# The sample's norm in each FFN taken apart around the plain products, and the last norm's first half of columns squared and weighted during the second half's products

## The chip, the cores and the metric

One core of one Trainium2 chip runs the whole program in one launch. The metric is the device time of an execution in microseconds, as the median of several executions of the same program.

## The reference

One inference step of a small streaming encoder for two groups of requests: a prompt of 512 tokens and a sample of 8 x 16 = 128 tokens, 1024 columns each, all in float32. Two layers: the first mixes with stick-breaking attention and gated linear attention, the second with banded softmax attention over a cache. After each mixer stands an FFN, and at the end a last norm. What matters here:

```python
def _rmsnorm(x, g):
    xf = x.astype(jnp.float32)
    y = xf * lax.rsqrt(jnp.mean(xf * xf, axis=-1, keepdims=True) + EPS)
    return (y * g.astype(jnp.float32)).astype(x.dtype)

def _swiglu(h, wg, wu, wd):
    return (jax.nn.silu(h @ wg) * (h @ wu)) @ wd
...
        xp = xp + _swiglu(_rmsnorm(xp, norm_ffn_g[layer]), w_ffn_gate[layer], w_ffn_up[layer],
                          w_ffn_down[layer]).astype(xp.dtype)
        xs = xs + _swiglu(_rmsnorm(xs, norm_ffn_g[layer]), w_ffn_gate[layer], w_ffn_up[layer],
                          w_ffn_down[layer]).astype(xs.dtype)

    y_prompt = _rmsnorm(xp, norm_final_g)
    y_sample = _rmsnorm(xs, norm_final_g)
```

The hidden width of the FFN (`D_FF`) is 2816.

## The kernel before

**Tiling.** The 640 tokens are five blocks of 128 rows: blocks 0 to 3 are the prompt, block 4 is the sample. `xt[b]` is the residual stream of block b, as two halves of 512 columns. For a product, the normalised rows are transposed on TensorE and kept by columns: `fT[kp]`, four tiles of two chunks of 128 of the 1024 columns, each with all 640 tokens. Float32 products are made of three products of rounded halves: `split` (L286) makes a high part `wh` on ScalarE (L289) and a low part `wl` on VectorE (L290), in four buffers each, and every product is `wh` by high, `wh` by low, `wl` by high (L692 to L694 in the FFN's first part, L323 to L325 in its second).

**A norm.** `rstd_of` (L230) squares both halves of a block on ScalarE into a junk tile `sqj` and adds them up by row (L235), then a Newton step on VectorE with `Ln` and `Exp` on ScalarE between (L240 to L244) gives `r`. `norm_block` (L247) scales the rows by `r` into `h`, the first half on VectorE and the second on GpSimd (L252), transposes them with eight matmuls against an identity matrix into `tp` (L255), and scales each of the eight chunks by its `gm` into `fT`, turn about on ScalarE (L263) and VectorE (L261).

**The FFN.** `ffn` (L738) takes the hidden columns in groups of 6, 6, 6 and 4 chunks. In a group, `fast_pair` (L670) handles 256 columns of a weight matrix with a Strassen-like scheme: seven products of sums instead of eight. `operand` (L644) builds the sums of the activations (tiles `xs`, L657) and splits them (`block`, L660; `xb` or `xt`, L664 on ScalarE and L665 on VectorE); `weights` (L697) builds the sums of the weights, `sw`, on GpSimd (L699). A block named `b11` or `b21` holds the first 320 tokens, `b12` or `b22` the last 320, in which block 4, the sample, lies. The first two fast pairs of each FFN (the gate and the up matrix for the first 256 hidden columns, `mats[0]` and `mats[1]`) are not done in the fast way but by plain products, `part(0)` for the first 320 tokens and `part(1)` for the last 320 (L679; accumulators `pb`, copied out at L750 and L763). Between them stands `last_norm`, the norm of the sample's block, whose rows come late out of `out_sample` (L616; its adds into `x` are L626). Its transposes are queued on TensorE behind the last matmul of `mats[1]`'s `part(0)`. After the plain products follow `mats[2]`'s products (`py`, `px`, `pq`).

The FFN's second part, `proj_as` (L312), multiplies by `w_ffn_down` and adds into `xt` (L813), one half of 512 columns after the other, for each group of hidden columns. In the last group the second half closes block by block (`tail=TAIL`), and then `after` is called for each block. In layer 1 this is `after1` (L1187): norm of the block, `y` from both halves on VectorE with `gf`, the last norm's weights times -0.5 (L1193), and a transfer of 512 KB to the output on SyncE's queue (L1194).

**Order.** Each engine runs its instructions in one fixed order. A planner makes that order when the program is built: it simulates the engines with durations of its own and gives a free engine the ready instruction with the lowest priority number, which is the place in the written program unless `priority` sets another. `tc.issue_after` adds a place in the order behind a given instruction. Work tiles come from pools: `ws` (six buffers) holds `sqj`, `h`, `xs` and the gate and up outputs `sg` and `up`.

Of the kernel before, what the change touches and what calls it, by code (L numbers as in the profile page):

```python
# [8 lines left out]
F32 = mybir.dt.float32  # L9
# [3 lines left out]
AF = mybir.ActivationFunctionType  # L13
ALU = mybir.AluOpType
PSUM = bass.MemoryType.PSUM

P = 128
D = 1024
NB = 5
# [23 lines left out]
TAIL = 4  # L43
# [6 lines left out]
GROUPS = (6, 6, 6, 4)  # L50
# [5 lines left out]
def kernel(  # L56
# [8 lines left out]
    nc = tc.nc  # L65
# [40 lines left out]
    t5 = tagged("t5", N5)  # L106
# [112 lines left out]
        fill=0.0, base=DS - 1, channel_multiplier=-1,  # L219
    )  # L220

    xs_flat = x_sample.rearrange("b t d -> (b t) d")

    def x_rows(src_p, src_s, b):
# [5 lines left out]
    def rstd_of(xt, sb=None):  # L230

        ss = small.tile([P, 2], F32, tag="ss", name="ss")
        for i in range(2):
            j = (sb or ws)([P, 512], "sqj")
            nc.scalar.activation(j, xt[i], AF.Square, scale=1.0 / 32.0, accum_out=ss[:, i:i + 1])  # L235
        v = small.tile([P, 1], F32, tag="rv", name="rv")
        r = small.tile([P, 1], F32, tag="rr", name="rr")
        a = small.tile([P, 1], F32, tag="ra", name="ra")
        V = nc.vector
        V.tensor_scalar(v, ss[:, 0:1], ss[:, 1:2], EPS, op0=ALU.add, op1=ALU.add)  # L240
        nc.scalar.activation(r, v, AF.Ln)
        last_exp[:] = [nc.scalar.activation(r, r, AF.Exp, scale=-0.5)]
        V.tensor_scalar(a, r, r, v, op0=ALU.mult, op1=ALU.mult)
        V.tensor_scalar(r, a, -3.0, r, op0=ALU.add, op1=ALU.mult)  # L244
        return r

    def norm_block(xt, gi, hT, b, sb=None, bank=None, after=None):  # L247
        r = rstd_of(xt, sb)
        for i in range(2):
            tp = (bank or za)([P, 4, P], "tp")  # L250
            h = (sb or ws)([P, 512], "h")
            scaled = (nc.vector, nc.gpsimd)[i].tensor_scalar(h, xt[i], r, -0.5, op0=ALU.mult, op1=ALU.mult)  # L252
            with tc.issue_after(after.ins) if after else nullcontext():
                for j in range(4):
                    nc.tensor.transpose(tp[:, j, :], h[:, j * P:(j + 1) * P], ident)  # L255
            for j in range(4):
                c = 4 * i + j
                if len(hT) == 4:
                    d = hT[c // 2][:, c % 2, b * P:(b + 1) * P]
                    if j % 2:  # L260
                        nc.vector.tensor_scalar(d, tp[:, j, :], gm[:, gi, c:c + 1], None, op0=ALU.mult)  # L261
                    else:
                        nc.scalar.activation(d, tp[:, j, :], AF.Copy, scale=gm[:, gi, c:c + 1])  # L263
                    continue
                H = hT[c][:, 0, b * P:(b + 1) * P]
                L = hT[c][:, 1, b * P:(b + 1) * P]
                g = gm[:, gi, c:c + 1]
                nc.scalar.activation(H, tp[:, j, :], AF.Copy, scale=g)
                nc.vector.scalar_tensor_tensor(
                    L, tp[:, j, :], g, H.bitcast(F32), op0=ALU.mult, op1=ALU.subtract)  # L270
        return scaled

    def new_hT(nm):
        return [t5([P, 2, NT], f"{nm}{c}", F32R) for c in range(8)]
# [460 lines left out]
            out(1, 0, st["Q"], st["U"])  # L735
        return head, body, tail, part

    def ffn(l, xt, fT, after, last_norm):  # L738
        X, comb, block = operand(fT)
        c0, silu = 0, []  # L740
        for gi, G in enumerate(GROUPS):
# [34 lines left out]
            for i, (head, body, tail, part) in enumerate(mats):  # L776
                if gi == 0 and i == 1:
                    continue
                if gi == 0 and i == 0:


                    block("b11")
                    block("b21")
                    part(0)
                    last_norm(mats[1][3](0))
                    block("b12", gt_)
                    block("b22")
                    part(1)
                    mats[1][3](1)
                    mats[2][0]()  # L790
                    comb("t3", "b22", "b12")
                    block("t3")
                    comb("t1", "b12", "b11")
                    comb("t2", "b22", "t1")
                    block("t2")
                    block("t1")
                    comb("t4", "b21", "t2")
                    block("t4")
                    continue
# [9 lines left out]
            for half in range(2):  # L809
                last = half == 1 and gi == len(GROUPS) - 1  # L810

                def ev(b, ps):
                    nc.vector.tensor_add(xt[b][half], xt[b][half], ps)  # L813
                proj_as(l, w_ffn_down[l][c0 * P:(c0 + G) * P, :], 512 * half, 512, gT, ev,
                        tail=TAIL if last else 1, after=after if last else None)
            c0 += G


# [290 lines left out]
        last_scaled[:] = [norm_block(xt[b], 2, hT2, b)]  # L1109
    stack.close()  # L1110
    with ffn_pools():
        ffn(0, xt, hT, after0, lambda mm: norm_block(xt[4], 1, hT, 4, after=mm))
    hT = hT2


# [68 lines left out]
    nc.sync.dma_start(gf, norm_final_g.unsqueeze(0).to_broadcast([P, D]))  # L1184
    nc.vector.tensor_scalar(gf, gf, -0.5, None, op0=ALU.mult)

    def after1(b):  # L1187
        r = rstd_of(xt[b])
        dst = y_prompt[0, b * P:(b + 1) * P, :] if b < 4 else y_sample.rearrange("b t d -> (b t) d")
        y = t5([P, D], "y")  # L1190
        for i in range(2):
            s = slice(512 * i, 512 * i + 512)
            nc.vector.scalar_tensor_tensor(y[:, s], xt[b][i], r, gf[:, s], op0=ALU.mult, op1=ALU.mult)  # L1193
        nc.sync.dma_start(dst, y)  # L1194
    stack.close()
    with ffn_pools():
        ffn(1, xt, hT, after1, lambda mm: norm_block(xt[4], 3, hT, 4, after=mm))


# [37 lines left out]
```

## Time and profile before

| | |
|---|---|
| Median of three executions | 1778.29 us (1778.0 to 1786.5) |
| The profiled execution | 1781.72 us, of which its span 1780.0 us |
| Mean granted TensorE clock | 0.979 |
| TensorE busy | 1697.9 us, 95% of the span |
| VectorE, ScalarE, GpSimd busy | 1108.4, 812.0, 317.7 us |
| Chain that ended last | PE 82%, DVE 11%, ACT 3%, issue 2%, DMA 2% |
| First half of FFN 0's plain products | from 439.80 us |
| First half of FFN 1's plain products | from 1321.03 us |
| Last matmul | 1768.15 us |

All times in the profile's rows count from the first instruction. In the rows, PE is TensorE's matmuls, PEld its loads of weights, DVE VectorE, ACT ScalarE, POOL GpSimd, SP SyncE, and a q behind an engine's name its queue. A row of a timeline has the start, the duration, the engine, the line of the kernel, the operation with output and inputs, shapes, and a count of like instructions in a row; in brackets stands how long the engine was idle before it and what ended that.

### The profile page before, as it was taken

The numbers are of one execution on the slowest core, as the hardware profiler recorded it, in microseconds if no ns is written. First come the engines' busy times: TensorE is split into PE (matmuls) and PEld (weight loads), VectorE is DVE, ScalarE is ACT, GpSimd is POOL, SyncE is SP. The second block draws the span as 40 slices with busy tenths as digits, with TensorE's granted clock in tenths as the row PEclk, the third lists the DMA queues.
The fourth block names the chain that finished last, engine by engine and source line by source line (L and its number), as shares of the span: only waits on it lengthen the run. The fifth ranks groups of instructions, "written<-read, shape, count | busy, mean of one in ns | idle before, by whom it ended". The sixth has DMA issues, their size and how long they took to land.

```text
span 1780.0 us, 31737 instructions
## 1 busy us (share of the span) xinstructions
PE 1697.9 (95%) x12520; PEld 1522.9 (86%) x12520; DVE 1108.4 (62%) x2237; ACT 812.0 (46%) x1805; POOL 317.7 (18%) x339
## 2 busy tenths in 40 slices
PE   7999999998889999999999999999787999999997
PEld 7898997896788998989898889888567889899896
DVE  6466586765684765856555654755647837658465
ACT  6454435455552543534454433534536525335253
POOL 2000000000241413414110000001104224043130
PEclk9999998999899999999999999999998999999999
DMA  5311131574122222222343233368822313222212
GB/s 144 97 56 49 56 97 54 186 244 155 59 77 90 71 96 71 73 95 70 122 134 99 83 96 108 116 211 300 311 98 62 105 60 95 83 83 73 93 60 83
DMA packets 157173, 192.09 MB, mean 108 GB/s; under 512 B 12976, under 2 KB 109248, under 8 KB 157024
## 3 DMA queue, kind: packets, MB, share of 16 engines
q1 hardware_dynamic: 153440, 178.40, 30.8%
q0 software_dynamic: 3584, 11.67, 2.1%
q8 instruction: 98, 1.61, 0.4%
q14 instruction: 51, 0.42, 0.1%
HBM read 175.75 MB, written 14.29 MB: 107 GB/s over the span
## 4 chain that ended last, share of the span: by engine, by line
PE 82%; DVE 11%; ACT 3%; issue 2%; DMA 2%; SPq 0%; DVEq 0%; ACTq 0%
PE pn L323 6%; PE pn L325 6%; PE pn L324 6%; PE pw L304 5%; PE pw L305 5%; PE pw L306 5%; DVE wl L290 3%; PE px L692 3%; PE px L693 3%; PE px L694 3%; PE kttp L535 2%; PE py L694 2%; PE pm L356 2%; PE pm L359 2%; PE pm L358 2%
## 5 line engine op out<-in xcount | busy, mean ns | idle before, releaser
L290 DVE TENSOR_TENSOR wl<-raw,wh 128x512 fp32r<-128x512 f32 (+1 forms) x370 | 289.0, 788 | 251.0 <-ACT wh L289 248.5
L289 ACT CAST wh<-raw 128x512 fp32r<-128x512 f32 (+1 forms) x370 | 227.8, 618 | 377.7 <-PE pn L325 163.4
L699 POOL TENSOR_TENSOR sw<-raw 128x512 f32<-128x512 f32 x80 | 128.5, 1610 | 533.2 <-DMA raw<-in_w_ffn_gate_dram 298.2
L324 PE MATMUL pn<-wl,gT 128*128 128x512 f32 x440 | 171.2, 389 | 0.0
L289 ACT CAST wh<-sw 128x512 fp32r<-128x512 f32 x160 | 99.4, 621 | 154.9 <-PE px L693 64.4
L325 PE MATMUL pn<-wh,gT 128*128 128x512 f32 x440 | 169.3, 389 | 0.0
L323 PE MATMUL pn<-wh,gT 128*128 128x512 f32 x440 | 166.8, 389 | 0.0
L290 DVE TENSOR_TENSOR wl<-sw,wh 128x512 fp32r<-128x512 f32 x160 | 120.7, 758 | 52.6 <-ACT wh L289 41.4
L694 PE MATMUL py<-xb,wl 128*128 128x320 f32 x320 | 100.6, 314 | 9.2 <-DVE wl L290 9.2
L694 PE MATMUL pq<-xt,wl 128*128 128x320 f32 x320 | 98.8, 310 | 4.0 <-DVE wl L290 4.0
L692 PE MATMUL pq<-xt,wh 128*128 128x320 f32 x320 | 99.1, 310 | 2.2 <-ACT wh L289 2.2
L692 PE MATMUL px<-xt,wh 128*128 128x320 f32 x320 | 98.9, 309 | 0.0
L693 PE MATMUL pq<-xt,wh 128*128 128x320 f32 x320 | 98.9, 309 | 0.0
L693 PE MATMUL px<-xt,wh 128*128 128x320 f32 x320 | 98.9, 309 | 0.0
L694 PE MATMUL px<-xt,wl 128*128 128x320 f32 x320 | 98.9, 309 | 0.0
L693 PE MATMUL py<-xb,wh 128*128 128x320 f32 x320 | 98.8, 309 | 0.0
L692 PE MATMUL py<-xb,wh 128*128 128x320 f32 x320 | 98.8, 309 | 0.0
L325 PEld LDWEIGHTS pn<-wh,gT 128*128 128x128 f32 x440 | 82.6, 188 | 16.9
L324 PEld LDWEIGHTS pn<-wl,gT 128*128 128x128 f32 x440 | 82.6, 188 | 16.9
L323 PEld LDWEIGHTS pn<-wh,gT 128*128 128x128 f32 x440 | 82.3, 188 | 16.6
L304 PE MATMUL pw<-hTa,wh 128*128 128x320 f32 (+1 forms) x272 | 89.9, 331 | 0.0
L305 PE MATMUL pw<-hTa,wh 128*128 128x320 f32 (+1 forms) x272 | 88.9, 327 | 0.0
(329 smaller groups left out, 4721.5 us busy)
## 6 DMA issues: line engine op xcount, KB each, us to landing
raw<-in_w_ffn_gate_dram SPq DMA_DIRECT2D x44, 512.0 KB, 3.8
raw<-in_w_ffn_up_dram SPq DMA_DIRECT2D x44, 512.0 KB, 3.7
raw<-in_w_ffn_down_dram SPq DMA_DIRECT2D x44, 512.0 KB, 3.3
kr<-in_cache_c_k_dram SPq DMA_DIRECT2D x64, 256.0 KB, 5.4
vr<-in_cache_c_v_dram SPq DMA_DIRECT2D x16, 1024.0 KB, 7.0
raw<-in_w_in_ab_dram SPq DMA_DIRECT2D x24, 512.0 KB, 3.8
raw<-in_w_qkv_c_dram SPq DMA_DIRECT2D x24, 512.0 KB, 3.8
vr<-in_cache_a_v_dram SPq DMA_DIRECT2D x8, 1024.0 KB, 5.6
```

Of the source, the lines that this page charges most:

```text
L289: nc.scalar.copy(H, rawv)
L290: nc.vector.tensor_sub(L, rawv, H.bitcast(F32))
L304: MM(ps[i], lhsT=H[:, k % 4, :], rhs=hT[k][:, 0, s], start=(k == 0), stop=False)
L305: MM(ps[i], lhsT=H[:, k % 4, :], rhs=hT[k][:, 1, s], start=False, stop=False)
L306: MM(ps[i], lhsT=L[:, k % 4, :], rhs=hT[k][:, 0, s], start=False, stop=(k == 7))
L323: MM(ps[b], lhsT=lhs[k][:, 0, bs], rhs=H, start=(k == 0), stop=False)
L324: MM(ps[b], lhsT=lhs[k][:, 0, bs], rhs=L, start=False, stop=False)
L325: MM(ps[b], lhsT=lhs[k][:, 1, bs], rhs=H, start=False, stop=(k == K - 1))
L692: MM(ps, lhsT=H[:, k, :], rhs=X[x][0][k], start=(first and k == 0), stop=False, **f)
L693: MM(ps, lhsT=H[:, k, :], rhs=X[x][1][k], start=False, stop=False, **f)
L694: last = MM(ps, lhsT=L[:, k, :], rhs=X[x][0][k], start=False, stop=(k == 3), **f)
L699: nc.gpsimd.tensor_tensor(t, a, b, op=op)
```

## The change

**The sample's norm in each FFN.** `rstd_of` gives its second part to a function `newton`. `norm_block` is taken apart into `norm_rows` (squares, Newton step, scaling by `r`) and `norm_columns` (transposes and scaling by `gm`). In `ffn`, `last_norm` is now a pair: the rows are written ahead of `block("b11")` and of all plain products, with both halves scaled on VectorE (`ROWS`) rather than one on GpSimd; the columns are written behind `mats[0]`'s `part(0)`, with the transposes queued behind its last matmul, so that `mats[1]`'s `part(0)` stands between the transposes and the splits of `b12` and `b22`. Both FFNs have this.

**The last norm.** A new function `half1` is called for each block in layer 1 when the first half of 512 columns of the last group is added: it squares that half and multiplies it in place by `gf`. `after1` squares the second half and does the Newton step. The output is written for all five blocks behind the last block's Newton step: the first half by a scaled copy on ScalarE, the second by one instruction on VectorE, both in place, with a transfer of 256 KB for each half rather than one of 512 KB for both.

```diff
+    ROWS = (nc.vector, nc.vector)
...
+        newton(ss, r)
+        return r
+
+    def newton(ss, r):
         v = small.tile([P, 1], F32, tag="rv", name="rv")
...
-    def norm_block(xt, gi, hT, b, sb=None, bank=None, after=None):
+    def norm_rows(xt, sb=None, engines=None):
+
         r = rstd_of(xt, sb)
+        hs = []
         for i in range(2):
+            h = (sb or ws)([P, 512], "h")
+            scaled = (engines or (nc.vector, nc.gpsimd))[i].tensor_scalar(
+                h, xt[i], r, -0.5, op0=ALU.mult, op1=ALU.mult)
+            hs.append(h)
+        return hs, scaled
+
+    def norm_block(xt, gi, hT, b, sb=None, bank=None):
+        hs, scaled = norm_rows(xt, sb)
+        norm_columns(hs, gi, hT, b, bank)
+        return scaled
+
+    def norm_columns(hs, gi, hT, b, bank=None, after=None):
+
+        for i, h in enumerate(hs):
             tp = (bank or za)([P, 4, P], "tp")
-            h = (sb or ws)([P, 512], "h")
-            scaled = (nc.vector, nc.gpsimd)[i].tensor_scalar(h, xt[i], r, -0.5, op0=ALU.mult, op1=ALU.mult)
             with tc.issue_after(after.ins) if after else nullcontext():
...
                 if gi == 0 and i == 0:
+                    rows = last_norm[0]()
                     block("b11")
                     block("b21")
-                    part(0)
-                    last_norm(mats[1][3](0))
+                    last_norm[1](rows, part(0))
+                    mats[1][3](0)
                     block("b12", gt_)
                     block("b22")
                     part(1)
...
                 proj_as(l, w_ffn_down[l][c0 * P:(c0 + G) * P, :], 512 * half, 512, gT, ev,
-                        tail=TAIL if last else 1, after=after if last else None)
+                        tail=TAIL if last else 1,
+                        after=after if last else first_half if gi == len(GROUPS) - 1 else None)
...
+    def final(nm, n=1):
+        return [small.tile([P, n], F32, tag=nm, bufs=NB, name=nm) for _ in range(NB)]
+
+    ssf, rf = final("ssf", 2), final("rf")
+
+    def square(b, i):
+        j = ws([P, 512], "sqj")
+        nc.scalar.activation(j, xt[b][i], AF.Square, scale=1.0 / 32.0, accum_out=ssf[b][:, i:i + 1])
+
+    def half1(b):
+
+        square(b, 0)
+        nc.vector.tensor_mul(xt[b][0], xt[b][0], gf[:, :512])
+
     def after1(b):
-        r = rstd_of(xt[b])
-        dst = y_prompt[0, b * P:(b + 1) * P, :] if b < 4 else y_sample.rearrange("b t d -> (b t) d")
-        y = t5([P, D], "y")
-        for i in range(2):
-            s = slice(512 * i, 512 * i + 512)
-            nc.vector.scalar_tensor_tensor(y[:, s], xt[b][i], r, gf[:, s], op0=ALU.mult, op1=ALU.mult)
-        nc.sync.dma_start(dst, y)
+        square(b, 1)
+        newton(ssf[b], rf[b])
+        if b < NB - 1:
+            return
+        for b in range(NB):
+            dst = y_prompt[0, b * P:(b + 1) * P, :] if b < 4 else y_sample.rearrange("b t d -> (b t) d")
+            x = xt[b]
+            nc.scalar.activation(x[0], x[0], AF.Copy, scale=rf[b])
+            nc.sync.dma_start(dst[:, :512], x[0])
+            nc.vector.scalar_tensor_tensor(x[1], x[1], rf[b], gf[:, 512:], op0=ALU.mult, op1=ALU.mult)
+            nc.sync.dma_start(dst[:, 512:], x[1])
     stack.close()
     with ffn_pools():
-        ffn(1, xt, hT, after1, lambda mm: norm_block(xt[4], 3, hT, 4, after=mm))
+        ffn(1, xt, hT, after1, (lambda: norm_rows(xt[4], engines=ROWS)[0],
+                              lambda rows, mm: norm_columns(rows, 3, hT, 4, after=mm)), half1)
```

Layer 0's call of `ffn` changes in the same way, without `half1`.

More of the change, by code (lines that the diff above doesn't have):

```diff
@@ L235, in rstd_of @@
             nc.scalar.activation(j, xt[i], AF.Square, scale=1.0 / 32.0, accum_out=ss[:, i:i + 1])
+        r = small.tile([P, 1], F32, tag="rr", name="rr")
+        newton(ss, r)
+        return r
+    def newton(ss, r):
         v = small.tile([P, 1], F32, tag="rv", name="rv")
-        r = small.tile([P, 1], F32, tag="rr", name="rr")
         a = small.tile([P, 1], F32, tag="ra", name="ra")
@@ L244, in rstd_of @@
         V.tensor_scalar(r, a, -3.0, r, op0=ALU.add, op1=ALU.mult)
-        return r
-    def norm_block(xt, gi, hT, b, sb=None, bank=None, after=None):
+    def norm_rows(xt, sb=None, engines=None):
         r = rstd_of(xt, sb)
+        hs = []
         for i in range(2):
+            h = (sb or ws)([P, 512], "h")
[9 more added lines that the diff above has]
+        for i, h in enumerate(hs):
             tp = (bank or za)([P, 4, P], "tp")
-            h = (sb or ws)([P, 512], "h")
-            scaled = (nc.vector, nc.gpsimd)[i].tensor_scalar(h, xt[i], r, -0.5, op0=ALU.mult, op1=ALU.mult)
             with tc.issue_after(after.ins) if after else nullcontext():
@@ L270, in norm_block @@
                     L, tp[:, j, :], g, H.bitcast(F32), op0=ALU.mult, op1=ALU.subtract)
-        return scaled
     def new_hT(nm):
@@ L736, in fast_pair, with ffn @@
         return head, body, tail, part
-    def ffn(l, xt, fT, after, last_norm):
+    def ffn(l, xt, fT, after, last_norm, first_half=None):
         X, comb, block = operand(fT)
@@ L1111 @@
     with ffn_pools():
-        ffn(0, xt, hT, after0, lambda mm: norm_block(xt[4], 1, hT, 4, after=mm))
+        ffn(0, xt, hT, after0, (lambda: norm_rows(xt[4], engines=ROWS)[0],
+                              lambda rows, mm: norm_columns(rows, 1, hT, 4, after=mm)))
     hT = hT2
```

## The prediction

> **What bounds the kernel now.** I read the page first, then the timeline of each engine around the two places that the change touches, then sums by stretch, then the waits of the tail.
>
> ```profile
> span 1780.0 us, 31737 instructions
> PE 1697.9 (95%) x12520; PEld 1522.9 (86%) x12520; DVE 1108.4 (62%) x2237; ACT 812.0 (46%) x1805; POOL 317.7 (18%) x339
> PE 82%; DVE 11%; ACT 3%; issue 2%; DMA 2%; SPq 0%; DVEq 0%; ACTq 0%
> ```
>
> TensorE is busy 95% of the span and is 82% of the chain that ended last: only time in which it stands, or runs at less than its full clock, can be won. The change touches three such places. The first two are alike, one in each FFN. TensorE's timeline there (start, duration, line, tiles, count, and in brackets the idle time before it with what ended it), FFN 1 above FFN 0:
>
> ```profile
> 1335.21 0.31 PE L693 MATMUL pb<-xb,wh 128*128 128x320 f32 x1
> 1335.36 0.31 PE L694 MATMUL pb<-xb,wl 128*128 128x320 f32 x1
> 1340.58 1.97 PE L255 MATMUL tp<-ident,h 128*128 128x128 f32 x8 [4.91 <-DVE h L252]
> 1343.81 0.90 PE L692 MATMUL pb<-xb,wh 128*128 128x320 f32 x2 [1.26 <-ACT xb L664]
> 1346.60 0.64 PE L693 MATMUL pb<-xb,wh 128*128 128x320 f32 x1 [1.89 <-DVE xb L665]
> ...
> 439.01 1.04 PE L255 MATMUL tp<-ident,h 128*128 128x128 f32 x8
> 459.57 1.94 PE L255 MATMUL tp<-ident,h 128*128 128x128 f32 x8 [4.95 <-DVE h L252]
> ```
>
> The plain products of both matrices for the first 320 tokens end; TensorE waits 4.91 us for the sample's normalised rows `h`, transposes them, waits 1.26 and 1.89 us for the splits `xb`, and only then goes on. In sums (length, busy time and count of PE, PEld, DVE, ACT, POOL, granted clock), first half of the plain products, standstill and second half, first for FFN 1, then for FFN 0, there with the stretch behind them:
>
> ```profile
> 1321.03:1335.67 14.64, 14.63 (x98) 14.13 (x96) 5.53 (x8) 5.43 (x11) 0.00 (x0) 1.00 0.00 0
> 1335.67:1362.15 26.48, 18.42 (x106) 17.62 (x107) 17.54 (x28) 15.98 (x34) 6.36 (x5) 0.81 0.26 80
> ...
> 439.80:454.61 14.81, 14.81 (x99) 14.07 (x97) 8.15 (x15) 8.17 (x18) 0.00 (x0) 1.00 0.00 1
> 454.61:481.31 26.70, 18.57 (x107) 17.79 (x107) 17.52 (x28) 15.99 (x34) 6.36 (x5) 0.81 0.26 79
> 481.31:510.70 29.39, 24.04 (x158) 22.99 (x158) 29.16 (x38) 17.25 (x34) 20.63 (x8) 1.00 0.17 54
> ```
>
> The two halves are the same 96 matmuls, yet the first takes 14.7 us and the second, with 8 transposes, 26.5 and 26.7 us, partly at half clock (0.81 on the mean). The third place is the end of the kernel.
>
> **The norm in each FFN.** Why is `h` late? The inputs and what ran between, FFN 1, then FFN 0:
>
> ```profile
> 1321.63 0.69 DVE L626 TENSOR_TENSOR x<-x,ps 128x512 f32<-128x512 f32 x1 [1.39 <-PE ps L625]
> 1323.23 0.62 ACT L289 CAST wh<-raw 128x512 fp32r<-128x512 f32 x1 [4.60 <-PE pb L693]
> 1336.08 0.42 ACT L763 COPY up<-pb 128x320 f32<-128x320 f32 x1
> 1336.40 0.63 ACT L235 ACTIVATE sqj<-x 128x512 f32<-128x512 f32 x1
> 1339.11 1.41 DVE L252 TENSOR_SCALAR h<-x,rr 128x512 f32<-128x512 f32 x1
> 1341.73 0.37 ACT L263 ACTIVATE fT<-tp,gm 128x128 f32<-128x128 f32 x1 [3.28 <-PE tp L255]
> 1344.67 2.62 DVE L665 TENSOR_TENSOR xb<-fT,xb 128x640 fp32r<-128x640 f32 x2
> 1347.58 0.72 ACT L664 CAST xb<-fT 128x640 fp32r<-128x640 f32 x1 [2.32 <-DVE fT L261]
> ...
> 439.21 0.69 DVE L626 TENSOR_TENSOR x<-x,ps 128x512 f32<-128x512 f32 x1 [6.18 <-PE ps L625]
> 441.14 2.17 ACT L289 CAST wh<-raw 128x512 fp32r<-128x512 f32 x4
> ```
>
> The sample's rows are whole at 1321.63 + 0.69 = 1322.32, but ScalarE squares them at 1336.40, behind the last `up` copy, though it stood idle 4.60 us just ahead of 1323.23. Nothing but the written order holds them. The change writes squares, Newton step and both scalings ahead of the products. The same steps took 1336.40 to 1340.52 (end of `h` on VectorE); begun at 1322.3 they end near 1326.5 even at that pace. The transposes now follow the first matrix's 48 products, which end about 1321.0 + 7.3 = 1328.3: `h` is there. So the 4.91 us go. Behind the transposes stand the second matrix's 48 products, 48 x 0.147 us (from one start to the next, 1335.21 to 1335.36) = 7.05 us. They cover the 8 scalings by `gm`, one after another on ScalarE and VectorE at 0.37 = 3.0 us, and the four splits `xb`; the last leaves VectorE some 3.0 + 0.72 + 2 x 0.82 = 5.4 us after the transposes, so 1.26 and 1.89 us go too. Without a standstill the clock stays up: the transposes cost 1.04 us as at 439.01, not 1.97, and the second half 96 x 0.147 = 14.1 us. The stretch becomes 15.1 us against 26.48 and 26.70: 11.4 and 11.6 us won, 23.0 together.
>
> What it costs: in FFN 0 the rows are whole only at 439.90, when TensorE is already at its products; the second square (0.63, some 0.7 with its read-out) goes ahead of the four casts at 441.14, and the products wait for those: up to 0.7 us; I take 0.6. In FFN 1 the idle 4.60 us cover the squares: nothing. Scaling the second half of the rows moves from GpSimd to VectorE: one more 0.5 us there, hidden in the first half, where VectorE works 5.5 to 8.2 of 14.7 us. VectorE is what may give something back. From 439.80 to 510.70 it works 8.15 + 17.52 + 29.16 = 54.8 us, and in the last 29.39 us it has no idle time at all. With 11.6 us less the whole is 59.3 us long. VectorE sheds about 1.6 us of lengthened instructions as they no longer run beside GpSimd (by the 0.69 of the adds on 512 columns, two `xb` on 640 are 1.7 where 2.62 stand, and `h` 0.7 where 1.41 stands): 53.2 us. Against that stands idle time that it can't use, waiting in order for weight buffers that TensorE frees: half of its 6.7 idle us in the first half (3.3) and of its 9.2 in the second stretch (4.6): 59.3 - 7.9 = 51.4. So 1.8 us return per FFN; bounds 0 (that idle time is used) and 5 (below, first rival). I take 1.5 each, since some of it will be used: 23.0 - 0.6 - 3.0 = 19.4 us.
>
> GpSimd forms the sums `sw` of the first fast pair (the second row gives the least, median and longest in ns, and the first start):
>
> ```profile
> L699 POOL TENSOR_TENSOR sw<-raw 128x512 f32<-128x512 f32 x80 | 128.5, 1610 | 533.2 <-DMA raw<-in_w_ffn_gate_dram 298.2
> ...
> L699 POOL TENSOR_TENSOR sw<-raw x80: 1261/1301/9826, 457.9 to 1718.8; 128x512 f32<-128x512 f32 x80
> 454.12 2.12 SPq L676 DMA_DIRECT2D raw<-in_w_ffn_gate_dram  x2
> ```
>
> Today these run while TensorE stands; afterwards they run beside the second half. The transfer is issued 0.5 us before the first half ends and the first sum begins 3.8 us later, at 457.9; they are needed some 17.6 us after it (14.1 plus 24 products at 0.147), so at 1.3 us each they are hidden. The Trainium skill, "SBUF — State Buffer", section "Who interferes with whom", speaks against this: a VectorE instruction with two SBUF inputs and a GpSimd instruction that reads SBUF exclude each other, and the later one waits for the whole of the earlier one. By that rule alone each sum would wait for one VectorE instruction, an estimate of 1.3 + 0.8 = 2.1 us, still hidden, and the sum would stay. The 9.826 us of the slowest row is far more than one instruction's wait; so the row, not the rule, prices the last rival.
>
> **The end.**
>
> ```profile
> 1761.55 0.69 DVE L813 TENSOR_TENSOR x<-x,pn 128x512 f32<-128x512 f32 x1 [5.01 <-PE pn L325]
> 1762.27 0.63 ACT L235 ACTIVATE sqj<-x 128x512 f32<-128x512 f32 x1 [6.62 <-DVE x L813]
> 1767.37 2.73 DVE L1193 SCALAR_TENSOR_TENSOR y<-x,rr,gf 128x512 f32<-128x512 f32 x4
> 1768.15 0.39 PE L325 MATMUL pn<-wh,gT 128*128 128x512 f32 x1
> 1770.26 0.68 DVE L813 TENSOR_TENSOR x<-x,pn 128x512 f32<-128x512 f32 x1
> 1772.79 0.21 DVE L240 TENSOR_SCALAR rv<-ss 128x1 f32<-128x1 f32 x1
> ...
> L1194 SPq DMA_DIRECT2D out_dram<-y x5: 332/333/357, 1768.8 to 1776.2; - x5
> ```
>
> The last product ends at 1768.54 (1768.15 + 0.39), but the last block's add comes at 1770.26 and its `rv` at 1772.79, each behind VectorE's scalings of other blocks; the last transfer is issued at about 1776.2, 7.7 us after the product. Five first-half squares (5 x 0.7) and five products with `gf` (5 x 0.69, by the adds) move into ScalarE's 6.62 and VectorE's 5.01 idle us: nothing, unless they delay the second half's last weight split, by four squares at most, 2.9 us, which other blocks' products cover. VectorE's scalings halve, five instead of ten; ScalarE takes the other five (0.62, as its casts of that shape) and is idle there. The last block then needs add 0.7, square 0.8, `rv` 0.25, Ln and Exp 0.5, two Newton steps 0.6, scaling 0.7 (2.73 for four) = 3.6 us, and I add 1.1 for one or two other instructions in VectorE's queue: 4.7 against 7.7, so 3.0 us won. Ten transfers of 256 KB replace five of 512; five more issues at 0.333 us are 1.7 us of SyncE, most of them while products still run. Bounds: 4.1 won (no interference), 1.0 lost (the written order, all output behind the last block's norm, bunches scalings and transfers).
>
> **Sum.** 19.4 + 3.0 = 22.4 us. The profiled execution took 1781.72 us (span 1780.0 and 1.7 around it); 1759.3 after. It stands 3.4 above the median of the three runs, 1778.29: predicted 1756.
>
> **Rivals.** *Splits come late.* As the squares did before, `xb` could stand behind the two `up` copies in ScalarE's queue, since the planner decides by its own durations, and these copies wait for the end of the second matrix's products. The splits then begin when the first half ends. Today 5.75 us pass from the end of the transposes (1342.55) to the end of the last `xb` cast (1348.30), some of them scalings by `gm`: I take 5 us of standstill. For it: ScalarE would have 6.5 us of work in the 7.05. Against: the scalings by `gm` are written ahead of that matrix's splits. Time: 6.4 won less per place than 11.4, 2 x 6.4 - 0.6 + 3.0 = 15.2: 1763.
>
> *The rows are not done earlier.* If the planner holds the squares for another reason than the written order, such as a work buffer, only the end is won: 1775. Against: the idle 4.60 us, and the same place behind the `up` copy in both FFNs.
>
> *Slower: GpSimd starves.* One sum took 9.826 us instead of 1.301, in the stretch where VectorE never paused. The first three sums of each FFN are now beside busier VectorE work. They have some 12 us to spare, so one such wait (8.5 us) is absorbed. Three (25.6) overrun by 13.4 us; less 9.7 won that is 3.7 lost per FFN, minus 3.0 at the end: 4.4 lost, 1783. It decides against the change from about 22 us of waiting in three sums. Against: (1610 - 1301) x 80 ns are 24.7 us of lengthening in all, not three such waits among 80 sums, and VectorE has idle time in the second stretch now (9.2 us) which it keeps in part.
>
> **How the numbers follow.** Forecast 0.62, late splits 0.20, rows not earlier 0.07, starved 0.06, and 0.05 for the planner laying out other work anew for better or worse. The range goes from 27 won (both places whole, the end at its best), 1751, less 1 for the runs' scatter, to the late splits with nothing won at the end, 1766, and 1 more. A measurement tells 0.5%, 8.9 us, from no change: faster needs 1769.4 or less. Forecast, late splits and 0.02 of the rest give faster 0.84; rows not earlier and 0.02 give same 0.09; slower 0.07.
>
> **What would show it.** Right: in both FFNs squares begin within a few us of the last add into the sample's rows; transposes start without idle time after 48 plain products; 96 more follow with no waits over 1 us; the granted clock is 1.00 there; the stretches of 26.5 us are near 16. At the end, the last add follows the last product within 1 us and the last issue comes 4 to 5 us after it. Wrong: TensorE idle ahead of a product that reads the second half's `xb`; an `sw` of several us; idle time growing in the 29 us behind; or a mixer stage of other length.

## The result, and the profile after

The changed kernel takes 1766.44 us (median of five executions, 1761.2 to 1770.83); the kernel before, timed beside it, 1779.81 (five executions). The ratio is 0.9911 with a 95% interval of 0.9885 to 0.9937: faster by 13.4 us by the two medians and by 15.8 by the ratio, which is not that of the medians; 22.4 were forecast. The profile below is that of the slowest of the five (1770.83 us, span 1769.1); it has 10.9 us less than the profiled execution of before. Two of the forecast's three terms came out as worked out. The difference lies in a stage of which the prediction says nothing, and at the end.

The page of the changed kernel, the same three lines as shown of before:

```profile
span 1769.1 us, 31748 instructions
...
PE 1702.8 (96%) x12520; PEld 1518.2 (86%) x12520; DVE 1110.4 (63%) x2239; ACT 814.3 (46%) x1810; POOL 314.0 (18%) x337
...
PE 82%; DVE 10%; DMA 3%; ACT 2%; issue 2%; SPq 0%; DVEq 0%; ACTq 0%
```

The first surprise stands in the second line: TensorE does the same 12520 matmuls, the standstills are gone, and yet it is busy for longer (1702.8 us against 1697.9).

TensorE's timeline of the changed kernel at the two places, FFN 1 above FFN 0:

```profile
1324.86 0.31 PE L711 MATMUL pb<-xb,wl 128*128 128x320 f32 x1
1325.01 1.04 PE L273 MATMUL tp<-ident,h 128*128 128x128 f32 x8
1325.81 0.39 PE L709 MATMUL pb<-xb,wh 128*128 128x320 f32 x1
...
440.76 0.41 PE L709 MATMUL pb<-xb,wh 128*128 128x320 f32 x1 [0.51 <-DVE rr L249]
...
442.29 0.41 PE L711 MATMUL pb<-xb,wl 128*128 128x320 f32 x1 [0.45 <-DVE wl L307]
...
447.09 1.04 PE L273 MATMUL tp<-ident,h 128*128 128x128 f32 x8
```

After 48 products the transposes run at once, in 1.04 us, and the next products follow without idle time. The 4.91, 1.26 and 1.89 us of before are gone; in FFN 0 two waits of half a microsecond have come, at the first products. ScalarE and VectorE show why, here in FFN 1:

```profile
1318.17 0.69 DVE L643 TENSOR_TENSOR x<-x,ps 128x512 f32<-128x512 f32 x1 [1.26 <-PE ps L642]
1318.89 0.63 ACT L236 ACTIVATE sqj<-x 128x512 f32<-128x512 f32 x1 [1.82 <-DVE x L643]
1320.93 0.88 DVE L257 TENSOR_SCALAR h<-x,rr 128x512 f32<-128x512 f32 x2
1330.09 1.55 DVE L682 TENSOR_TENSOR xb<-fT,xb 128x640 fp32r<-128x640 f32 x2
```

The square starts 0.03 us after the last add into the sample's rows; `h` is whole at 1321.81, 3.2 us ahead of the transposes; the last split ends at 1331.64, still before the 48 products of the second matrix do (1325.81 + 7.05 = 1332.9).

In sums (length, busy time and count of PE, PEld, DVE, ACT, POOL, granted clock, DMA share, GB/s) for all 192 plain products with the transposes and for the stretch behind them, up to the first product with `w_ffn_down`. Of the kernel before, FFN 0's two stretches and then FFN 1's:

```profile
439.80:481.14 41.34, 33.20 (x203) 31.69 (x202) 25.50 (x42) 24.10 (x50) 6.36 (x5) 0.88 0.17 52
481.14:535.70 54.56, 48.89 (x326) 47.58 (x325) 47.98 (x68) 31.29 (x61) 26.61 (x12) 1.00 0.24 78
1321.03:1361.99 40.96, 32.89 (x203) 31.59 (x202) 22.91 (x35) 21.36 (x43) 6.36 (x5) 0.88 0.17 52
1361.99:1416.58 54.59, 48.88 (x327) 47.56 (x325) 48.01 (x68) 31.30 (x61) 26.66 (x12) 1.00 0.24 78
```

and of the changed kernel, in the same order:

```profile
438.25:469.06 30.81, 29.86 (x203) 29.10 (x202) 24.27 (x42) 21.83 (x46) 5.64 (x4) 1.00 0.22 60
469.06:526.75 57.69, 51.48 (x327) 49.11 (x325) 49.57 (x69) 32.08 (x64) 25.34 (x12) 0.97 0.25 79
1317.57:1346.99 29.42, 29.42 (x202) 29.18 (x201) 21.79 (x34) 19.11 (x39) 5.64 (x4) 1.00 0.21 58
1346.99:1402.16 55.17, 50.31 (x326) 47.56 (x325) 49.59 (x70) 32.48 (x65) 26.42 (x12) 1.00 0.28 85
```

The plain products win 10.53 and 11.54 us at a granted clock of 1.00; the stretches behind give back 3.13 and 0.58 us, FFN 0's at a clock of 0.97. Then comes the rest of each FFN, where the program hardly differs. Here is FFN 0's, before and after, each first as a whole and then for the 660 products `pn` with `w_ffn_down` alone (of these, PE, PEld, DVE):

```profile
535.70:887.97 352.27, 350.15 (x2020) 322.92 (x2019) 217.38 (x337) 146.98 (x285) 97.15 (x75) 1.00 0.26 85
535.70:887.97 352.27, 151.08 (x660) 123.45 (x660) 24.91 (x39) 1.00 0.26 85
```

```profile
526.75:882.81 356.06, 353.92 (x2020) 323.01 (x2019) 217.23 (x337) 146.99 (x285) 96.41 (x75) 1.00 0.27 84
526.75:882.81 356.06, 154.65 (x660) 123.57 (x660) 24.85 (x39) 1.00 0.27 84
```

The same instructions on every engine, the clock at 1.00, the idle time of TensorE the same (352.27 - 350.15 = 2.12; 356.06 - 353.92 = 2.14), and 3.79 us more, of which 3.57 are in the 660 `pn` products. FFN 1's rest has 5.06 more. From one start to the next, `pn` takes 226.9 ns on the mean before and 232.3 after: 5.4 ns times 1320 products are 7.1 us of the 8.85 by which the two rests grew; another 0.9 is idle time of TensorE in FFN 1's rest (2.79 us, before 1.85). The products on 320 columns keep their 147 ns.

With 1.51 us won behind the last matmul, 1.55 won ahead of FFN 0 and 1.71 lost in the mixer between the FFNs the account is whole: 22.07 - 3.71 - 8.85 + 1.51 + 1.55 - 1.71 = 10.86 us, the difference of the spans. The two stretches outside the FFNs scatter by several us from execution to execution, whatever the kernel (434.5 to 442.6 and 429.7 to 438.0 us in the profiles of this study), so single profiles say nothing about a few us there.

### The profile page after: what moved, and what is told of

It reads as the page before. It is cut to its first block, busy times and chain, and to the rows that moved or that the text cites. A ratio compares the mean times of both kernels' runs of the same rounds, so it can differ in the third digit from the quotient of the medians.

```text
span 1769.1 us, 31748 instructions
## 1 busy us (share of the span) xinstructions
PE 1702.8 (96%) x12520; PEld 1518.2 (86%) x12520; DVE 1110.4 (63%) x2239; ACT 814.3 (46%) x1810; POOL 314.0 (18%) x337
## 3 DMA queue, kind: packets, MB, share of 16 engines
q8 instruction: 98, 1.61, 0.4%
## 4 chain that ended last, share of the span: by engine, by line
PE 82%; DVE 10%; DMA 3%; ACT 2%; issue 2%; SPq 0%; DVEq 0%; ACTq 0%
PE pn L340 6%; PE pn L342 6%; PE pn L341 6%; PE pw L321 5%; PE pw L322 5%; PE pw L323 5%; DVE wl L307 4%; PE px L710 3%; PE px L709 3%; PE px L711 3%; PE py L711 2%; PE kttp L552 2%; PE pm L373 2%; DMA kr<-in_cache_c_k_dram 2%; PE pm L376 2%; PE pm L375 2%
## 5 line engine op out<-in xcount | busy, mean ns | idle before, releaser
L342 PE MATMUL pn<-wh,gT 128*128 128x512 f32 x440 | 171.5, 394 | 0.0
L340 PE MATMUL pn<-wh,gT 128*128 128x512 f32 x440 | 168.9, 395 | 0.0
L321 PE MATMUL pw<-hTa,wh 128*128 128x320 f32 (+1 forms) x272 | 88.5, 325 | 0.0
L323 PE MATMUL pw<-hTa,wl 128*128 128x320 f32 (+1 forms) x272 | 87.8, 323 | 0.0
```

Source lines behind the costliest of these rows:

```text
L321: MM(ps[i], lhsT=H[:, k % 4, :], rhs=hT[k][:, 0, s], start=(k == 0), stop=False)
L323: MM(ps[i], lhsT=L[:, k % 4, :], rhs=hT[k][:, 0, s], start=False, stop=(k == 7))
L340: MM(ps[b], lhsT=lhs[k][:, 0, bs], rhs=H, start=(k == 0), stop=False)
L342: MM(ps[b], lhsT=lhs[k][:, 1, bs], rhs=H, start=False, stop=(k == K - 1))
```

## The experiments

Two things were to be explained: the slower `pn`, and the small gain at the end. For the first, the suspect (A in the expectations) was the place of tiles in SBUF: the ten small tiles `ssf` and `rf` lie below the FFN's stage pool and, by the addresses of the compiled programs, move all of it up by 320 bytes, the `gT` tiles in it (the stationary operand of `pn`) from 180416 to 180736; the weight halves `wh` and `wl` do not move. The rivals were that the last norm's new work in FFN 1 slows the products, or that the five executions were unlucky ones. For the end, the suspects were the ten issues (D) and the 2.6 MB of output (E).

### The change again, its two halves alone, and the place alone

`after_again` is the changed kernel once more. 

> The changed kernel once more. In its profile the 512-column products of the FFNs' second part (tile pn) start 232.3 ns apart on the mean, against 226.9 before: 1320 of them, 7.1 us. Theory A (place): the ten small tiles of the last norm move all tiles of the FFN stage up by 320 bytes, and the products pay for the place of their operands: 232 ns again, about 0.9911 of before. Theory B (state of the execution): the pitch differs from execution to execution: it may be 227 here, and then the profiled span is about 7 us shorter, near 1762.

`ffn_only` keeps the norm in the FFNs and puts back the last norm:

```diff
-    ssf, rf = final("ssf", 2), final("rf")
...
-        square(b, 1)
-        newton(ssf[b], rf[b])
...
+        r = rstd_of(xt[b])
...
+            nc.vector.scalar_tensor_tensor(y[:, s], xt[b][i], r, gf[:, s], op0=ALU.mult, op1=ALU.mult)
+        nc.sync.dma_start(dst, y)
```

> The two norms in the FFNs as in the changed kernel, the end as before; no small tile is added, so the FFN stage lies where it lay before. Theory A: pitch of pn 227 ns; the two stretches win 10.5 and 11.5 us, about 3.7 us return behind them: 18 us won, 0.990 or a little less, that is as fast as the changed kernel or 1 to 5 us faster, although the end is the old one. Theory B: pitch 227 or 232 as it falls; on the median 1.5 us slower than the changed kernel.

`end_only` keeps the last norm and puts back the norm in the FFNs:

```diff
...
-                    rows = last_norm[0]()
                     block("b11")
                     block("b21")
-                    last_norm[1](rows, part(0))
-                    mats[1][3](0)
+                    part(0)
+                    last_norm(mats[1][3](0))
...
```

> The last norm as in the changed kernel, the FFNs' norms as before; the FFN stage lies 320 bytes further up. Theory A: pitch of pn 232 ns, 7.1 us lost and some 1.5 won at the end: 1.003 of before. Theory B: pitch as it falls, the median 1.5 us below before: 0.999. The prediction had 3.0 us for this part alone: 0.998.

`pad320` is the kernel before with an unused tile of 320 bytes:

```diff
+    gap = ctx.enter_context(tc.tile_pool(name="gap", bufs=1)).tile([P, 80], F32, name="gap")
+    nc.gpsimd.memset(gap, 0.0)
```

> The kernel before with one unused tile of 320 bytes ahead of the FFN stage's tiles, and nothing else but one instruction on GpSimd at the start that fills it. Theory A: pitch of pn 232 ns, 1.004 of before, 7 us slower. Theory B: as before, 1.000, with a pitch that falls as it falls.

Measured, beside 1782.48 us for the kernel before (23 executions):

| | median us | ratio, 95% interval | `pn`, start to start |
|---|---|---|---|
| after_again | 1766.41 | 0.991 (0.989 to 0.9929) | 232.3 ns |
| ffn_only | 1760.64 | 0.9879 (0.9856 to 0.9901) | 226.9 ns |
| end_only | 1786.15 | 1.0021 (1.0008 to 1.0033) | 232.3 ns |
| pad320 | 1786.52 | 1.0023 (1.001 to 1.0036) | 232.3 ns |

The costliest groups (line, engine, operation, tiles, count, then busy us, mean ns of one and idle us) have a row for each of the three products; of `ffn_only`:

```profile
L341 PE MATMUL pn<-wl,gT 128*128 128x512 f32 x440 | 171.2, 389 | 0.0
```

and of `pad320`, which has no other change than the unused tile:

```profile
L326 PE MATMUL pn<-wl,gT 128*128 128x512 f32 x440 | 173.7, 395 | 0.0
```

(A single matmul's end is modelled, so the row shows the difference and not the length.) The result of the change is no accident of five executions; the last norm's work is not what slows `pn`; 320 unused bytes do the same to the kernel before. The place is the cause. The changed kernel shows it within one execution, too: the `gT` tiles of every second group's first pair come from `t5`, which lies outside the stage pool and was not moved. Fifteen products in a row that read such a tile, and then the fifteen that follow and read a tile of the stage (length, busy time and count of PE, PEld and DVE for `pn`):

```profile
531.95:535.35 3.40, 3.40 (x16) 2.82 (x15) 0.00 (x0) 1.00 0.48 154
535.35:538.85 3.50, 3.50 (x16) 2.82 (x15) 0.00 (x0) 1.00 0.20 49
```

Without the displacement, the norm in the FFNs alone wins 21.8 us. The last norm alone loses 3.7, and 0.4 less than the unused tile; by the means it is 1.2 less, and twelve executions of each scatter too much to tell these from the 1.5 of the profiles. The profiles agree with one another: behind the last matmul stand 11.40 to 11.76 us in the five with the old end and 9.75 to 10.08 in the eight with the new one and all of its output. One thing does not fit: `pad320` lost 4.0 us in the median, not 7.1. Its profile, of the second longest of twelve executions (1790.99 us), is 9.3 us longer than before's, 8.6 of them in the two FFNs' rests; why the median lost less is open.

### The change without the displacement, and one transfer for a block

`after_place` is the changed kernel with the ten small tiles in buffers that were there already, so that the stage pool lies where it lay:

```diff
...
-    ssf, rf = final("ssf", 2), final("rf")
+    ssf, rf = final("ssf", 2, "m", "bl"), final("rf", 1, "tot", "ebl")
```

> The changed kernel, with the ten small tiles of the last norm in buffers that the attention's softmax and the linear attention have left, so that nothing is added ahead of the FFN stage and its tiles lie where they lay before. Instructions as in the changed kernel. Theory A (place): pitch of pn 227 ns, 7 to 8 us faster than the changed kernel, about 0.987 of before, and 1.5 us faster than the norms in the FFNs alone. Rival C (the moved tiles cost something else as well, or the end costs time elsewhere): pitch 227 but no faster than 0.990.

`one_out` does in addition one transfer of 512 KB for a block instead of two of 256:

```diff
...
+        whole[b] = t
...
-            nc.sync.dma_start(dst[:, :512], x[0])
...
-            nc.sync.dma_start(dst[:, 512:], x[1])
+            nc.sync.dma_start(dst, whole[b])
```

> As the kernel with the tiles in their old place, but one transfer of 512 KB for each block behind both of its scalings, rather than two of 256 KB. Theory D (issues): at the end ten issues on SyncE's queue stand one behind another, the last 0.5 to 0.8 us after the last scaling; with five, the stretch from the last matmul's end to the end of the span shrinks from 9.95 us to about 9.0. Rival E (bytes): the transfers themselves are the limit, and the stretch stays at 9.9 or grows, since the first halves leave later. On the median the difference is under the measurement's scatter.

Beside 1783.26 us for before (10 executions) `after_place` takes 1759.6 us, ratio 0.9871 (0.9851 to 0.9891): 23.7 us faster, 0.4% faster than the change as it was. Its stretch in FFN 0 is back at before's length:

```profile
526.60:878.94 352.34, 350.39 (x2020) 322.87 (x2019) 216.90 (x337) 146.93 (x285) 96.68 (x75) 1.00 0.26 85
```

`one_out` takes 1760.48 us, ratio 0.9872 (0.9851 to 0.9894), and from the end of the last matmul to the end of the span 9.96 us against 9.94: with half the issues the end is as long as it was. The five transfers begin 0.3 us later and run at 393 to 414 GB/s while the DMA engines are full, where the changed kernel's ten run at 371 to 391. D falls.

### Which half of the norm's change brings the gain

`rows_only` is `ffn_only` with the columns (transposes, `gm`) put back behind both matrices' first halves; only the rows are done early:

```diff
-                    last_norm[1](rows, part(0))
-                    mats[1][3](0)
+                    part(0)
+                    last_norm[1](rows, mats[1][3](0))
```

> The norms in the FFNs in half: the rows ahead of the products as in the changed kernel, but transposes and scalings by gm behind both matrices' first halves, as before; the end as before. If both halves of the change bear the gain as the prediction has it, the wait of 4.9 us for h goes and the two waits for xb stay, so the plain stretch is about 35 to 36 us where it was 41 and is 30.8 and 29.4: about half of the 21.8 us. If the early rows alone do it, it is near 31; if only the place of the columns does it, near 41.

1769.59 us, ratio 0.9933 (0.991 to 0.9957). The plain products take 35.12 and 33.76 us, between before's 41 and the change's 30. TensorE's waits in FFN 1 of this kernel:

```profile
1324.85 1.04 PE L273 MATMUL tp<-ident,h 128*128 128x128 f32 x8
1327.61 0.56 PE L709 MATMUL pb<-xb,wh 128*128 128x320 f32 x2 [1.72 <-ACT xb L681]
...
1328.67 0.41 PE L710 MATMUL pb<-xb,wh 128*128 128x320 f32 x1 [0.50 <-DVE xb L682]
...
1332.01 0.41 PE L710 MATMUL pb<-xb,wh 128*128 128x320 f32 x1 [1.31 <-DVE xb L682]
```

The transposes no longer wait, but the splits come late, since nothing covers them. So early rows are worth 6.2 and 7.2 us, and the second matrix's products between transposes and splits another 4.3 in each FFN, 8.6 in all; by the medians, each beside its own kernel before, it is 8.2 (`ffn_only` wins 21.84 us, `rows_only` 13.67). This also shows what the rival "splits come late" would have looked like.

### Which places are slow

Four kernels asked what it is about the place. `ladder` is `ffn_only` with each of the six `gT` buffers 64 bytes longer, by 8 elements in each half:

```diff
-                gt = [(t5 if gi % 2 == 0 and c == c0 else gt_)([P, 2, NT], "gT", F32R) for _ in range(2)]
+                gt = [(t5([P, 2, NT], "gT", F32R) if gi % 2 == 0 and c == c0 else gt_([P, 2, NT + 8], "gT", F32R)[:, :, :NT])
+                      for _ in range(2)]
```

> The norms in the FFNs as changed, the end as before, and the six buffers of gT in the FFN stage made 64 bytes longer each, so that they begin 192, 256, 320, 384, 448 and 0 bytes past a multiple of 512, and the low parts in them 224, 288, 352, 416, 480 and 32. One profile then shows the pitch of the 512-column products for each place of the operand that is loaded as weights; the gT tiles outside the stage, all at 192, are the control (227 to 228 ns in both kernels). Theory A1: the pitch goes by the place modulo 512, 227 at 192 and 233 at 0, with others between or at one of the two. Theory A2: it goes by something coarser (the distance to the moving operand, the absolute place), and the six buffers are alike, all near 227 or all near 233.

All six were slow (231.5 to 233.8 ns), even the one whose address is that of the kernel before. So the absolute place of the tile isn't the rule. But the low half of each lay 32 bytes off the high half's place, which the design had overlooked; the run decides nothing more. (1772.49 us in one execution.)

`pads` is `after_place` with unused bytes at the bottom of the stage pool, 512 in layer 0 and 256 in layer 1; `all320` is `after_place` with everything moved by 320 bytes, `gT` and the weight halves alike:

```diff
+    pads = [128, 64]
...
+            pad = m.tile([P, pads.pop(0)], F32, tag="pad", bufs=1, name="pad")
+            nc.gpsimd.memset(pad, 0.0)
```

```diff
+    gap = const.tile([P, 80], F32, name="gap")
+    nc.gpsimd.memset(gap, 0.0)
```

> The kernel with the tiles in their old place, and an unused tile at the bottom of the FFN stage: 512 bytes in layer 0, 256 bytes in layer 1 (one GpSimd instruction in each fills it). The streamed operand stays at 192 past a multiple of 512; gT lies at 192 in layer 0 and at 448 in layer 1. If the place counts modulo 512 (or a divisor), layer 0 has 227 ns; if coarser, both have about 233. If it counts modulo 256 or less, both have 227.

> The kernel with the tiles in their old place, and an unused tile of 320 bytes ahead of all work tiles, so that the operand loaded as weights (gT, in and outside the FFN stage) and the streamed one (wh, wl) move together from 192 to 0 past a multiple of 512. Theory A3 (the two operands' places relative to each other): pitch of pn 227 ns everywhere. Theory A4 (the place by itself): 233 ns, the gT tiles outside the stage included, which never were slow so far.

In one execution each, 1763.75 and 1755.33 us, beside 1779.25 for before. `pn` takes 226.9 ns in both, in `pads` in both layers. `all320` has `gT` at the same place as the changed kernel and yet before's pace, since the weights have moved along: the distance of the two operands counts, and distances of 0 and 256 bytes are free. (`pads` is 8.4 us slower than `all320`, 6.4 of them in the parts outside the FFNs; that is within their scatter.)

`steps64` repeats the ladder on `after_place`, with the halves of each tile 2560 bytes apart as ever, so that the six buffers lie 0 to 320 bytes from `wh` and `wl`, counted within 512:

```diff
-                gt = [(t5 if gi % 2 == 0 and c == c0 else gt_)([P, 2, NT], "gT", F32R) for _ in range(2)]
+                gt = [t5([P, 2, NT], "gT", F32R) if gi % 2 == 0 and c == c0 else
+                      gt_([P, 2 * NT + 16], "gT", F32R)[:, :2 * NT].rearrange("p (i t) -> p i t", i=2) for _ in range(2)]
```

> The version with the ten small tiles put elsewhere, with each of the six gT buffers of the FFN stage 64 B longer (high and low part now stay 2560 B apart), so that they lie 0, 64, 128, 192, 256 and 320 B (mod 512) from the weight halves wh and wl; 180 products of the second part read each. Theory R1 (a product is slowed unless its two operands lie a multiple of 256 B apart): buffers at 0 and 256 B 226.8 ns from start to start, the four others 231 to 236. Theory R2 (only some distances cost, among them 320): 320 at 233, 0 and 256 at 226.8, at least one of 64, 128, 192 at 226.8 too. Theory R3 (not the distance within 512 B counts, but that the buffers are no longer a multiple of 512 B apart): all six at 230 to 236. Time: 4 of 6 buffers slow are some 720 products x 5.4 to 6.6 ns = 3.9 to 4.8 us more than 1759.6, 1763 to 1765 by R1; by R3 5.8 to 7.1 more, 1765 to 1767.

Fifteen products in a row read one buffer. Such runs of fifteen, at distances of 0, 64, 128, 192, 256 and 320 bytes in this order (length, then busy time and count of PE, PEld and DVE for `pn`; a product that overlaps an edge is counted too):

```profile
1640.96:1644.36 3.40, 3.40 (x17) 2.82 (x16) 0.00 (x0) 1.00 0.19 59
1410.72:1414.22 3.50, 3.50 (x16) 2.82 (x15) 0.00 (x0) 1.00 0.24 92
1414.22:1417.71 3.49, 3.49 (x17) 2.83 (x16) 0.00 (x0) 1.00 0.23 75
1417.71:1421.15 3.44, 3.44 (x17) 2.82 (x15) 2.03 (x4) 1.00 0.20 76
1407.32:1410.72 3.40, 3.40 (x16) 2.82 (x15) 0.00 (x0) 1.00 0.18 59
1644.36:1647.86 3.50, 3.50 (x17) 2.82 (x15) 0.00 (x0) 1.00 0.24 92
```

Over all such runs without a pause in them (6, 10, 8, 6, 12 and 8) the means are 226.9, 233.2, 232.5, 229.4, 227.3 and 233.4 ns. 0 and 256 bytes are alike, and so are 64 and 320: the cost goes by the distance within 256, nothing at 0, 6.4 ns at 64, 5.6 at 128, 2.5 at 192. R1 holds, but 192 costs less than it had said; R2 and R3 fall. The whole kernel took 1765.74 us in one execution, 1782.72 for before beside it.

### What binds the end

`half_bytes` is `after_place` without the transfers of the output's first 512 columns; these 1.3 MB and five issues are left out:

```diff
             nc.scalar.activation(x[0], x[0], AF.Copy, scale=rf[b])
-            nc.sync.dma_start(dst[:, :512], x[0])
```

> The kernel with the tiles in their old place, without the transfers of the first half of columns of the last norm's output: 1.3 MB of 2.6 MB and five of ten issues are left out, all the arithmetic stays. Theory E (bytes): the transfers bind the end, since they start only when the last product is done; the stretch from the last matmul's end to the span's end shrinks from 9.94 us to about 8.6, where the last scaling, its issue and landing take over. Rival F (the last block's chain of norm and scaling binds it): it stays at 9.9.

From the last matmul's end to the span's end it has 8.3 us, against 9.94 with all the output (1755.77 us in one execution). That is 3.2 us less than before's 11.45, about what was forecast for the end. With half the bytes the transfers run as the scalings release them, the last one issued 4.9 us after the last product and landed some 2 us later; in this kernel the issues and transfers of the second halves are:

```profile
L1232 SPq DMA_DIRECT2D out_dram<-x x5: 332/332/356, 1745.8 to 1750.7; - x5
...
DMA to landing us min/median/max: 2.0/2.0/2.3
```

With all the bytes, the DMA engines (next to last column their busy share, last GB/s) hardly pause. In the changed kernel they are full from 1760.0, soon after the first issue (1759.16), until 1767.1, but for one us at 0.87:

```profile
1759.00:1760.00 1.00, 0.19 (x1) 0.00 (x0) 1.00 (x5) 1.00 (x3) 0.00 (x0) 1.00 0.00 0
1760.00:1761.00 1.00, 0.00 (x0) 0.00 (x0) 0.87 (x3) 1.00 (x6) 0.00 (x0) 1.00 1.00 371
...
1762.00:1763.00 1.00, 0.00 (x0) 0.00 (x0) 1.00 (x4) 0.85 (x3) 0.00 (x0) 0.50 0.87 313
...
1766.00:1767.00 1.00, 0.00 (x0) 0.00 (x0) 0.00 (x0) 0.00 (x0) 0.00 (x0) 0.50 1.01 383
1767.00:1768.00 1.00, 0.00 (x0) 0.00 (x0) 0.00 (x0) 0.00 (x0) 0.00 (x0) 0.50 0.08 27
```

In the kernel before, they stood half idle in between, in these two us above all:

```profile
1772.00:1773.00 1.00, 0.00 (x0) 0.00 (x0) 1.00 (x4) 0.00 (x0) 0.00 (x0) 1.00 0.26 102
1773.00:1774.00 1.00, 0.00 (x0) 0.00 (x0) 1.00 (x3) 0.41 (x2) 0.00 (x0) 0.60 0.30 119
```

E holds: 2.62 MB at some 375 GB/s are 7.0 us, and they begin only when the last product is done.

## Why the prediction was right or wrong

**The standstill in each FFN: right.** 23.0 less 0.6 were forecast, 22.07 were won. Each step is there: squares behind the last add, `h` before the transposes, transposes in 1.04 us behind 48 products, splits under the second matrix's 48 products, the clock at 1.00. The second square ahead of FFN 0's casts was put at 0.6; FFN 0's stretch is 1.39 us longer than FFN 1's where before it was 0.38 longer, so it cost 1.0.

**Given back behind: right in sum.** 1.5 for each FFN were forecast with bounds 0 and 5; 3.13 and 0.58 came (1.22 and 2.08 in `ffn_only`, 1.57 twice in `after_place`). The cause named is VectorE, and it is without idle time in the 29.44 us behind FFN 0's plain products (third sum of engines). TensorE does 149 products there, against 158 in the 29.39 us of before; nine of them at 147 ns are 1.3 us:

```profile
469.06:498.50 29.44, 23.80 (x149) 21.69 (x148) 29.44 (x38) 17.81 (x36) 19.92 (x8) 1.00 0.21 64
```

The rest of FFN 0's 3.13 us is something that the prediction did not have: the granted clock is 0.51 on the mean from 498.20 to 501.70, behind a wait of 1.83 us for `wl`, an estimate of 3.5 x 0.49 = 1.7 us lost. Why it fell just here is open: before, waits of 2.00 and 1.64 us in this stretch left it at 1.00. In `after_place`, where TensorE waits 1.61 us at that place and the clock stays at 1.00, the two FFNs give back 3.14 us together, near the 3.0 of the forecast.

**The rival of the starved GpSimd: did not come.** GpSimd's timeline in FFN 0:

```profile
458.90 1.30 POOL L716 TENSOR_TENSOR sw<-raw 128x512 f32<-128x512 f32 x1 [28.11 <-DMA raw<-in_w_ffn_gate_dram]
...
463.96 1.62 POOL L716 TENSOR_TENSOR sw<-raw,sw 128x512 f32<-128x512 f32 x1
472.81 9.11 POOL L716 TENSOR_TENSOR sw<-raw 128x512 f32<-128x512 f32 x1 [7.22 <-DVE wl L307]
```

The first pair's sums now run beside the plain products and take 1.30 to 1.62 us, as in the prediction. One later sum takes 9.11 us in each FFN, much as one in each took 9.8 before.

**The end: right up to the transfers, wrong in its size.** 3.0 us were forecast, 1.5 won in the profiles. The steps were that the last block's norm ends sooner and the last transfer is issued 4.7 us after the last product. The last rows of VectorE and ScalarE, and the first and last issue:

```profile
1758.79 0.40 PE L342 MATMUL pn<-wh,gT 128*128 128x512 f32 x1
1759.30 0.68 DVE L831 TENSOR_TENSOR x<-x,pn 128x512 f32<-128x512 f32 x1
1763.26 0.75 DVE L1231 SCALAR_TENSOR_TENSOR x<-x,rf,gf 128x512 f32<-128x512 f32 x1
1759.16 0.36 SPq L1232 DMA_DIRECT2D out_dram<-x  x1
1764.56 0.95 SPq L1232 DMA_DIRECT2D out_dram<-x  x1
```

The last add comes 0.1 us after the last product and the last scaling ends 4.8 us after it, as forecast; the last issue is at 5.4 us. Of the 1.5 us that are missing, 0.7 lie ahead of that issue (5.4 for 4.7 us) and 0.8 behind it: from there to the end of the span it is 4.6 us, before 3.8. The step that failed is the one that let the transfers behind the scalings take no longer than before. All output is now scaled within 5 us of the last product, while it takes 7 to write; before, the issues were spread from 1768.8 to 1776.2, and the transfers had the gaps shown above. With half of the bytes left out, the last issue is at 4.9 us and the end at 8.3. The prediction's bound "bunches scalings and transfers" named this, and priced it as the end of a range where it was the likely case: 2.62 MB divided by the rate of the transfers could have been worked out.

**Not foreseen: where the new tiles lie.** The prediction read the change as instructions and waits. Its ten tiles of 32 bytes per partition cost 7.1 us by the products' pace, and 7.6 by the medians: without the displacement the change brings 23.7 us, with it 16.1 in `after_again`, each beside its own kernel before. The forecast of 22.4 less these 7.1 and the 1.5 missing at the end is 13.8. The medians say 13.4 here and 16.1 in `after_again`, the two profiles 10.9; all fit within the scatter, and how near 13.8 comes to 13.4 is chance.

So the time fell near the price of "splits come late" (1763) for an altogether different reason: the plain products show that this rival did not come, and the stage in which the time was lost stood on no list of signs. That 1766.44 lies within the stated range, whose upper end of 1767 came from that rival, is luck: the place of the tiles was in neither the sum nor the bounds.

## What to carry to other kernels

When a change adds or moves tiles, compare the pace of unchanged matmuls before looking for waits: a stage of the same instructions that grows with no more idle time and with the clock at 1.00 has slower instructions. Keep the start of the stationary operand a whole multiple of 256 bytes from the start of the streamed one, for products on 512 columns, or put small tiles where they move nothing. And before a tail is shortened, divide its output by the rate of its transfers; below that time only writing some of it earlier helps.

## What the runs showed of the hardware that was not expected

The pace of 128x512 products with a stationary operand of 128x128, both fp32r, depends on the distance of the two operands within 256 bytes of a partition: 226.9 ns at 0, 233.2 at 64, 232.5 at 128, 229.4 at 192, 227.3 at 256, 233.4 at 320. Products on 320 columns kept 147 ns in all these kernels. In the changed kernel this holds one distance other than 0, by the addresses of the compiled programs: the parts `xb` of `b12`, which are streamed, lie in the stage pool as well (`block("b12", gt_)`), so that the weights start 192 bytes past them within 256; the 96 products that read them kept 146 ns. No other distance was tried on 320 columns. The Trainium skill, "SBUF — State Buffer", section "Who interferes with whom", gives TensorE two read ports for its two operands, independent of each other; by that rule alone the place of one against the other would not matter. These runs differ from it by up to 6.5 ns a product, and the measurement decides. Why the distance matters is open: the trace shows the next product's weights being loaded while this one runs (PEld 2.82 us of 3.40 above), but no run separates a meeting of the two reads from other reasons.

The DMA engines writing the output move 371 to 391 GB/s at a busy share of 1.0 with ten transfers of 256 KB and 393 to 414 with five of 512 KB; the end was no shorter with the five (9.96 against 9.94 us), which begin 0.3 us later.
